# Eight or nine gather buffers beside three or two kept units of query weights

## The chip, the cores and the metric

The kernel runs on one core of a Trainium2 chip. The metric is the time of one execution on the device, in microseconds; the median of several runs is given.

## What is computed

Four decoder layers over 256 tokens of 1024 features, batch 1, all in float32. Each layer has a token mixer (HGRN2, FoX attention, Mamba-2 SSD, HGRN2 again) and then a PEER feed-forward: a query projection, a top-16 search over product keys, and 16 experts for each of 8 heads, each expert being one row of a table `u` and one row of a table `v`. The feed-forward is where the kernel spends its memory traffic:

```python
def peer_ffn(h, w_q, sub_keys, u_tab, v_tab):
    ...
        q = (xb @ w_q).reshape(M, PEER_HEADS, 2, PEER_HALF)
        s = jnp.einsum('mhcd,hckd->mhck', q, sub_keys).astype(jnp.float32)
        sv, si = lax.top_k(s, PEER_TOPK)
        ...
        idx = jnp.take_along_axis(cand_i, pos, axis=-1)
        gates = jax.nn.softmax(top_s, axis=-1)
        u = jnp.take(u_tab, idx, axis=0)
        v = jnp.take(v_tab, idx, axis=0)
        act = jax.nn.gelu(jnp.einsum('md,mhkd->mhk', xb, u).astype(jnp.float32), approximate=False) * gates
        return jnp.einsum('mhk,mhkd->md', act.astype(xb.dtype), v)
```

Every one of 256 tokens in 4 layers needs 8 x 16 rows of `u` and as many of `v`, 4 KB each.

## The kernel before

**Stages.** The tokens are two blocks of 128, so there are eight stages `s` (layer `s // 2`, block `s % 2`). In stage `s` the main loop (L1340) does the expert part of stage `s` in 64 pairs, and in between, a few instructions at a time, the "side" work that prepares stage `s + 1`: norm, mixer, norm, queries (`ready`, L1247). How much side work goes into each pair is paced by `SIDE` and `SPAN`.

**Gathers.** The host has joined `u` and `v` row by row, so one gather (`fetch`, L1210) brings 128 rows of 8 KB, 1 MB, by an indirect DMA that POOL issues, into one of `NGB` buffers `GB[n % NGB]`. A pair `i` uses gathers `2i` and `2i + 1`. For each, VectorE multiplies the `u` half with the repeated activations and sums (`dot`, L1221, in place in the buffer), ScalarE applies gelu and the gate (`spread`, L1227), and TensorE multiplies a diagonal-like 128x64 weight with the `v` half into the accumulator (L1241). With that matmul the buffer is free. `fetches(i)` (L1215), called at the head of pair `i`, issues all gathers up to number `2 i + NGB - 1`; on the chip each then waits for its buffer. There are 1024 gathers.

**Weights.** All other weights come in units of 1 MB (128 x 2048 floats) in one order, `stream` (L258), issued by SyncE in `loads` (L276): the mixer's units, then eight units `wq` of the layer's query weights, for each block again. A unit goes, first match, to a kept place if it is one of the first `NKEPT` query units of a layer, to a home, or to one of `NRAW` = 3 ring slots; when no slot is free, loading stops until a unit is used up (`half`, L314). A kept unit is loaded for the first block of a layer and found in place for the second, so it is read from memory once in a layer, any other query unit twice.

**Homes.** Before the first gather the gather buffers are empty, so some units of the start (numbers in `stream`; 20 to 27 are the query units of stage 0) are loaded there (`homes`, L265). A gather into such a buffer waits until TensorE has used the unit. The hand-written `order` (L267) tells in which order the first units are loaded.

**Memory.** Everything large lies in one arena (L181): `kept` takes `NKEPT` x 2048 floats of each partition and `gb` takes `NGB` x 2048.

**Engine helpers.** VectorE's instructions are all recorded at L203, most of ScalarE's at L216, matmuls of the projections at L238, transposes at L242.

Of the kernel before, what the change touches and what calls it, by code (L numbers as in the profile page):

```python
# [25 lines left out]
HALF = UNIT // 2  # L26
TOPK = 16
NQ = TOPK // 2
NGB = 8
NRAW = 3  # L30
MIX = 10464
STAGES = 2 * DEPTH
NKEPT = 3

FREE = {"hg": 0, "fox": 64 + 8 * T + 2 * D, "ssd": 352 + 4 * D + 96}
SPACE = 7 * D + P
# [128 lines left out]
def trunk(ctx: ExitStack, tc: tile.TileContext, d: dict, out: bass.AP):  # L165
# [14 lines left out]
    fst = cpool.tile([P, P + 8 * 2 * DEPTH], F32, name="fst")  # L180
    sizes = (("h", 2 * D), ("xT", D), ("XR", 2 * D), ("keys", UNIT), ("SS", 2048), ("mix", MIX), ("kept", NKEPT * UNIT),  # L181
             ("gb", NGB * 2 * D))
    arena = cpool.tile([P, sum(n for _, n in sizes)], F32, name="arena")
# [8 lines left out]
    SS = at_["SS"].rearrange("p (h c k) -> p h c k", h=8, c=2)  # L192
    GB = [at_["gb"][:, i * 2 * D:(i + 1) * 2 * D] for i in range(NGB)]
    mix = at_["mix"]
# [67 lines left out]
            stream += [(nm, i) for i in range(UNITS[KIND[l] if KIND[l] != "ssd" else "ssm"])]  # L262
            stream += [("wq%d" % l, i) for i in range(8)]

    homes = {3: GB[0], 4: GB[1], 17: GB[0], 18: GB[1], 19: GB[2], 23: GB[5], 24: GB[6]}  # L265
    homes.update({28 + i: mix[:, o:o + UNIT] for i, o in enumerate((SPACE, D, 3 * D))})
    order = [0, 1, 2, "rest", *range(3, 9), 23, 9, 10, 11, 24, 12, 13, 14, 22, 15, 16, "x", 17, 20, 18, 21, 19, "keys",  # L267
             "factors", 28, 25, "heads", 29, 26, 27, "states", 30]
# [7 lines left out]
    def loads():  # L276

        while order:
# [11 lines left out]
            else:  # L290
                nm, i = stream[u]
                keep = nm[0] == "w" and i < NKEPT
                if keep:
# [916 lines left out]
    def fetch(n):  # L1210
        (s, hh, q), g = pairs[n // 2], n % 2
        nc.gpsimd.indirect_dma_start(GB[n % NGB], None, d["uv"],  # L1212
                                     bass.IndirectOffsetOnAxis(ap=got[s, hh][0][:, g, q:q + 1], axis=0))

    def fetches(n):  # L1215

        while sent[0] < 2 * len(pairs) and sent[0] < 2 * n + NGB and pairs[sent[0] // 2][:2] in got:
            fetch(sent[0])
            sent[0] += 1

    def dot(i, g):  # L1221
        if g == 0:
            acts[i] = wk2.tile([P, 3, 2], F32, name="dots", bufs=4)
        u = GB[(2 * i + g) % NGB][:, 0:D]
        stt(u, u, 1.0, XR[:, g], op0=OP.mult, op1=OP.mult, accum_out=acts[i][:, 0, g:g + 1])

    def spread(i):  # L1227
# [10 lines left out]
        for e in range(2):  # L1238
            for g in range(2):
                v = GB[(2 * i + g) % NGB][:, D + e * 512:D + (e + 1) * 512]  # L1240
                nc.tensor.matmul(accs[s][e][g * 64:g * 64 + 64], dg[:, g], v, start=hh == 0 and q == 0,  # L1241
# [146 lines left out]
```

## Time and profile before

| | |
|---|---|
| median of 3 runs | 3226.96 us (3226.89 to 3229.7) |
| the profiled execution | 3229.51 us, of which the span of its instructions is 3227.4 us |
| mean granted TensorE clock | 0.897 |
| gathers (software queue) | 1073.81 MB in 147456 packets, 80.7% of the DMA engines' time |
| weights and the rest (hardware queue) | 247.23 MB in 35136 packets, 18.6% |
| query units loaded | 52 (38 into ring slots, 14 into the arena) |

The first gather is issued 118.1 us after the start of the span, the last at 3201.0 us. All rows with an arrow `out<-in` name tiles of the program; `arena<-in_uv,ix` is a gather. A row of the waits names the waiting engine, what it was about to do, what ended the wait, and the total in us, the times and the longest.

### The profile page before, as it was taken

Reading aid. Unit: us, or ns where it says so; the run is one execution under the profiler, and the core shown is the slowest. Engines: PE = TensorE matmul, PEld = TensorE weight load, DVE = VectorE, ACT = ScalarE, POOL = GpSimd, SP = SyncE. Lnnn points to the kernel's source line nnn. Section 1 sums busy time; section 2 is a strip of 40 time slices with the busy share of each in tenths; the row PEclk is TensorE's granted clock in tenths of the full one; section 3 lists DMA queues with packets and bytes.
Section 4 is the critical chain, followed back from the end, with each engine's and each line's share of the span. In section 5 each row is a group of like instructions: output and inputs, shape, how many; then the busy total and the mean of one; then the engine's idle time right before and its main releaser. Section 6 shows DMA issues by size and latency. Waiting matters only on the chain.

```text
span 3227.4 us, 30827 instructions
## 1 busy us (share of the span) xinstructions
PE 2482.3 (77%) x8604; PEld 1105.2 (34%) x8604; DVE 2117.9 (66%) x5583; ACT 1352.6 (42%) x3893; POOL 1178.7 (37%) x1030
## 2 busy tenths in 40 slices
PE   9888787777677786898778897778776777876565
PEld 4433233233233432344233443333323333332222
DVE  2576657566666866778567876576666667667764
ACT  3353334253334533477234673354433544333332
POOL 0243334333343433343333333343333433344442
PEclk9999898898889998999889998999988899887777
DMA  8899999999999999999999999999999999999997
GB/s 312 346 421 421 421 418 418 421 418 411 420 415 421 401 420 421 417 420 405 414 414 419 420 419 407 417 418 421 415 418 417 408 421 419 415 405 421 418 416 330
DMA packets 182760, 1322.99 MB, mean 410 GB/s; under 512 B 20288, under 2 KB 20672, under 8 KB 21824
## 3 DMA queue, kind: packets, MB, share of 16 engines
q0 software_dynamic: 147456, 1073.81, 80.7%
q1 hardware_dynamic: 35136, 247.23, 18.6%
q8 instruction: 71, 1.16, 0.1%
q14 instruction: 97, 0.79, 0.1%
HBM read 1319.90 MB, written 1.05 MB: 409 GB/s over the span
## 4 chain that ended last, share of the span: by engine, by line
DMA 57%; PE 15%; DVE 10%; issue 10%; ACT 4%; POOL 3%; POOLq 0%; SPq 0%; DVEq 0%; ACTq 0%
DMA arena<-in_uv,ix 57%; DVE arena L203 8%; PE acc L1241 8%; PE pj L238 5%; POOL arena L1212 3%; PE ps L238 2%; ACT dots L216 2%; ACT L216 1%; ACT dg L216 1%; PE ps L242 1%; ACT arena L216 0%; DVE eq L203 0%; DVE si L203 0%; DVE ti L203 0%; DVE af L203 0%
## 5 line engine op out<-in xcount | busy, mean ns | idle before, releaser
L203 DVE SCALAR_TENSOR_TENSOR arena<-arena 128x1024 f32<-128x1024 f32 (+3 forms) x1282 | 1321.7, 1048 | 910.7 <-DMA arena<-in_uv,ix 861.9
L1212 POOL DMA_INDIRECT arena<-in_uv,ix x1024 | 1176.6, 1149 | 2022.7 <-PE acc L1241 1437.8
L1241 PE MATMUL acc<-arena,dg 128*64 128x512 f32 x4096 | 1304.0, 724 | 720.7 <-ACT dg L216 719.0
L1241 PEld LDWEIGHTS acc<-arena,dg 128*64 128x64 f32 x4096 | 480.7, 156 | 1355.9 <-ACT dg L216 1043.9
L238 PE MATMUL pj<-raw,arena 128*128 128x512 f32 x1648 | 774.3, 612 | 5.2 <-DMA raw<-in_ssm 3.2
L216 ACT ACTIVATE dots<-dots 128x2 f32<-128x2 f32 x512 | 103.6, 202 | 1545.3 <-DVE arena L203 1544.5
L238 PEld LDWEIGHTS pj<-raw,arena 128*128 128x128 f32 x1648 | 302.3, 194 | 484.6 <-issue 467.1
L216 ACT ACT_TABLE_LOAD x325 | 417.0, 1283 | 6.7 <-DVE arena L203 0.8
L216 ACT ACTIVATE dg<-m,dots 128x64 f32<-128x64 f32 x1024 | 292.5, 333 | 0.0
L216 ACT ACTIVATE dots<-dots,gs 128x1 f32<-128x1 f32 x1024 | 245.6, 286 | 16.7
L238 PE MATMUL ps<-arena 128*128 128x128 f32 (+3 forms) x992 | 129.4, 287 | 1.8 <-ACT arena L1078 0.9
L238 PE MATMUL pj<-arena 128*128 128x512 f32 (+1 forms) x288 | 125.2, 582 | 0.3 <-DVE arena L203 0.3
L238 PEld LDWEIGHTS ps<-arena 128*128 128x128 f32 (+2 forms) x992 | 102.4, 168 | 67.1 <-issue 40.8
L242 PEld LDWEIGHTS ps<-fst,arena 128*128 128x128 f32 x568 | 67.2, 146 | 88.1 <-issue 43.4
L242 PE MATMUL ps<-fst,arena 128*128 128x128 f32 x568 | 91.5, 288 | 6.9 <-DVE arena L203 4.1
L216 ACT ACTIVATE arena<-arena 128x512 f32<-128x512 f32 (+3 forms) x132 | 67.7, 555 | 43.9 <-DVE arena L203 41.4
L203 DVE DVE_READ_ACCUMULATOR arena<-arena 128x1 f32 x1024 | 84.0, 82 | 0.0
L238 PEld LDWEIGHTS pj<-arena 128*128 128x128 f32 x288 | 53.1, 192 | 70.1 <-issue 58.8
L203 DVE FIND_INDEX8 si<-sv,arena 128x8 uint32<-128x128 f32 x256 | 69.7, 284 | 0.0
L203 DVE MAX8 sv<-arena 128x8 f32<-128x128 f32 x256 | 61.7, 282 | 10.4 <-ACT arena L1082 5.7
L238 PE MATMUL ps<-cst,arena 128*128 128x128 f32 (+3 forms) x288 | 66.8, 360 | 0.0
L203 DVE COPY gs<-ig 64x16 f32<-64x16 f32 (+1 forms) x256 | 52.5, 205 | 4.7
(113 smaller groups left out, 1227.2 us busy)
## 6 DMA issues: line engine op xcount, KB each, us to landing
raw<-in_hg SPq DMA_DIRECT2D x72, 1024.0 KB, 9.2
raw<-in_ssm SPq DMA_DIRECT2D x64, 1024.0 KB, 9.3
raw<-in_wq SPq DMA_DIRECT2D x38, 1024.0 KB, 9.6
raw<-in_fox SPq DMA_DIRECT2D x32, 1024.0 KB, 9.1
arena<-in_uv,ix POOLq DMA_INDIRECT x1024, 15.3
arena<-in_wq SPq DMA_DIRECT2D x14, 1024.0 KB, 14.9
arena<-in_hg SPq DMA_DIRECT2D x8, 1024.0 KB, 13.3
arena<-in_keys SPq DMA_DIRECT2D x4, 1024.0 KB, 9.3
```

Source lines behind the costliest of these rows:

```text
L203: return getattr(nc.vector, name)(o, *a, **k)
L216: nc.scalar.activation(o, i, f, **k)
L238: nc.tensor.matmul(o, w, m, start=start, stop=stop)
L242: nc.tensor.transpose(o, i, ident)
L1212: nc.gpsimd.indirect_dma_start(GB[n % NGB], None, d["uv"], bass.IndirectOffsetOnAxis(ap=got[s, hh][0][:, g, q:q + 1], axis=0))
L1241: nc.tensor.matmul(accs[s][e][g * 64:g * 64 + 64], dg[:, g], v, start=hh == 0 and q == 0, stop=hh == 7 and q == NQ - 1)
```

## The change

`NGB` goes from 8 to 9 and `NKEPT` from 3 to 2, so the arena keeps its size: 2048 floats of each partition go from `kept` to `gb`. The third query unit of each layer now goes through the ring of three slots in both blocks, and at the start, as number 22 of the stream, to a home in a gather buffer; the homes of units 23 and 24 move up by one buffer, as the program lists them.

```diff
-NGB = 8
+NGB = 9
 NRAW = 3
 MIX = 10464
 STAGES = 2 * DEPTH
-NKEPT = 3
+NKEPT = 2
...
-    homes = {3: GB[0], 4: GB[1], 17: GB[0], 18: GB[1], 19: GB[2], 23: GB[5], 24: GB[6]}
+    homes = {3: GB[0], 4: GB[1], 17: GB[0], 18: GB[1], 19: GB[2], 22: GB[5], 23: GB[6], 24: GB[7]}
```

## The prediction

> **What bounds the kernel now.** I read the top of the page, the DMA rate cut by stage, then the same view cut around the dips in that rate, and last how long a gather takes to land inside and outside a dip. The page first (section 2's rows are 40 equal slices of 80.7 us):
>
> ```profile
> span 3227.4 us, 30827 instructions
> PE 2482.3 (77%) x8604; PEld 1105.2 (34%) x8604; DVE 2117.9 (66%) x5583; ACT 1352.6 (42%) x3893; POOL 1178.7 (37%) x1030
> DMA  8899999999999999999999999999999999999997
> ...
> DMA packets 182760, 1322.99 MB, mean 410 GB/s; under 512 B 20288, under 2 KB 20672, under 8 KB 21824
> DMA arena<-in_uv,ix 57%; DVE arena L203 8%; PE acc L1241 8%; PE pj L238 5%; POOL arena L1212 3%; PE ps L238 2%; ACT dots L216 2%; ACT L216 1%; ACT dg L216 1%; PE ps L242 1%; ACT arena L216 0%; DVE eq L203 0%; DVE si L203 0%; DVE ti L203 0%; DVE af L203 0%
> ```
>
> No engine is busy more than 77%, the DMA engines are busy in every slice, and the chain that ends last spends 57% of the span in gathers. So the time is a start, the bytes divided by a rate, and a tail. The next view cuts the DMA-fed part into the eight stages; columns are the stretch, its length, the busy time of PE, PEld, DVE, ACT and POOL, the granted clock, the DMA share and GB/s.
>
> ```profile
> 132.00:511.00 379.00, 303.33 (x997) 127.38 (x999) 253.00 (x665) 156.47 (x452) 141.53 (x126) 0.90 1.01 420
> 511.00:895.00 384.00, 282.26 (x1011) 127.24 (x1009) 248.44 (x674) 151.02 (x473) 145.54 (x130) 0.89 1.01 417
> 895.00:1273.00 378.00, 288.99 (x1056) 132.23 (x1053) 254.24 (x674) 156.68 (x474) 147.55 (x129) 0.91 1.01 416
> 1273.00:1698.00 425.00, 344.68 (x1212) 155.52 (x1209) 299.91 (x823) 217.11 (x572) 150.82 (x127) 0.92 1.01 414
> 1698.00:2117.00 419.00, 345.71 (x1273) 159.62 (x1271) 298.41 (x812) 211.43 (x561) 151.21 (x129) 0.94 1.01 416
> 2117.00:2511.00 394.00, 299.19 (x1028) 130.29 (x1027) 254.58 (x653) 159.63 (x461) 146.52 (x130) 0.90 1.01 417
> 2511.00:2891.00 380.00, 296.87 (x1041) 129.47 (x1039) 254.03 (x653) 159.11 (x458) 151.52 (x130) 0.90 1.01 413
> 2891.00:3200.00 309.00, 188.15 (x527) 73.70 (x522) 206.29 (x505) 93.68 (x345) 134.30 (x122) 0.77 1.01 419
> ```
>
> An undisturbed stretch stands at 421 GB/s, which I take as the ceiling of this kernel's mix:
>
> ```profile
> 140.00:400.00 260.00, 211.32 (x699) 87.58 (x697) 175.71 (x468) 117.40 (x322) 95.63 (x84) 0.92 1.01 421
> ```
>
> Each stage's shortfall is its length times (421 - rate)/421: 0.9, 3.6, 4.5, 7.1, 5.0, 3.7, 7.2 and 1.5 us, together 33.5 us. That is everything that a better fed DMA can give back between 132 and 3200 us. Seven dips hold much of it:
>
> ```profile
> 700.00:760.00 60.00, 40.92 (x134) 18.14 (x134) 33.34 (x89) 20.14 (x70) 18.70 (x18) 0.86 1.00 409
> 1051.00:1104.00 53.00, 43.47 (x202) 22.77 (x201) 44.61 (x125) 35.64 (x100) 23.51 (x21) 0.94 0.99 392
> 1440.00:1540.00 100.00, 89.69 (x349) 42.59 (x348) 83.62 (x212) 66.83 (x155) 33.80 (x28) 0.95 1.00 403
> 1600.00:1640.00 40.00, 40.00 (x137) 16.60 (x137) 21.32 (x51) 12.31 (x43) 14.99 (x14) 1.00 1.00 405
> 1894.00:1961.00 67.00, 62.75 (x265) 31.28 (x265) 58.74 (x140) 50.31 (x113) 21.23 (x19) 0.95 0.99 399
> 2490.00:2562.00 72.00, 53.34 (x222) 25.00 (x222) 51.35 (x131) 35.47 (x98) 33.48 (x28) 0.88 1.00 404
> 2836.00:2861.00 25.00, 19.82 (x77) 8.47 (x75) 15.47 (x42) 7.64 (x27) 11.61 (x11) 0.93 0.95 366
> ```
>
> By the same formula they lack 1.7, 3.6, 4.3, 1.5, 3.5, 2.9 and 3.3 us, 20.8 us in 417 us; the other 12.7 us lie in small dips. How a gather lives in the quiet stretch (140 to 400 us) and, below it, in a dip (2490 to 2535 us): its issues, then issue to landing:
>
> ```profile
> L1212 POOL DMA_INDIRECT arena<-in_uv,ix x84: 932/937/1978, 144.2 to 395.0; - x84
> DMA to landing us min/median/max: 9.2/17.5/21.7
> ```
>
> ```profile
> L1212 POOL DMA_INDIRECT arena<-in_uv,ix x19: 932/938/1824, 2490.2 to 2534.6; - x19
> DMA to landing us min/median/max: 10.4/12.7/15.1
> ```
>
> In the quiet stretch a gather starts every 260/84 = 3.10 us, so eight buffers turn once in 24.8 us, of which 17.5 us are DMA: the data waits in a queue. Between 2490 and 2535 few weight loads compete, a gather starts every 45/19 = 2.37 us, eight turn in 18.9 us, and 12.7 us of that is DMA. The rest of the turn, some 6 to 7 us, is the way from landing through dot, gelu and matmul to the next issue. In a dip the ring is therefore too short: the DMA runs out of gathers to work on. What holds POOL before a gather over the whole run says the same:
>
> ```profile
> POOL arena L1212 <- PE acc L1241: 1437.8, 424, 9.2
> POOL arena L1212 <- DVE arena L203: 262.6, 74, 8.5
> POOL arena L1212 <- DVE ts L203: 13.6, 4, 5.1
> ```
>
> It waits for a buffer (the matmul of L1241 that reads it last); waits that end with the routing's own instructions are a few us.
>
> **The change part by part.**
>
> Added bytes. Each layer streams its eight query units twice, and a kept one is loaded once. With two kept, unit 2 is loaded again in the second pass of each of four layers: four loads more, 52 becoming 56. The loads and what a load is:
>
> ```profile
> raw<-in_wq SPq DMA_DIRECT2D x38, 1024.0 KB, 9.6
> arena<-in_uv,ix POOLq DMA_INDIRECT x1024, 15.3
> arena<-in_wq SPq DMA_DIRECT2D x14, 1024.0 KB, 14.9
> ```
>
> 1024 KB is 1.0486 MB, at 421 GB/s 2.49 us; four are +10.0 us, as nothing hides a byte where the DMA is the bound. If they fell wholly into dips they would cost 0, the lower end; the upper end is 10.0.
>
> [...] I use 2.49.
>
> Ninth buffer. The number of gathers (1024), their POOL instructions and the order of DVE, ACT and PE stay. One more gather is in flight whenever the DMA is the bound, and a stretch of busy engines must last 2.49 us longer before the DMA starves. Two ways to size it. First, at most one buffer per dip: min(shortfall, 2.49) over the seven is 1.7 + 2.5 + 2.5 + 1.5 + 2.5 + 2.5 + 2.5 = 15.7, and the small dips, each far under 2.49, return whole, 12.7: 28.4 us. Second, a dip limited by the ring alone speeds up by 9/8, capped at 421: 392 would be 441, 399 would be 449, only 366 stays below, at 412; nearly all 33 us return. Against both stand the stretches in which PE is itself the bound (40.00 of 40 us at 1600, 62.75 of 67 at 1894, 89.69 of 100 at 1440): the buffer shifts their start once and the engine is still full. I halve their 1.5 + 2.5 + 2.5 and take 28.4 - 3.3 = 25 us. The ends: 0 if one more buffer leads to no more in flight, 9.2 if only the four dips with PE under 85% return theirs and no small one does, 33.5 if all returns.
>
> Start. Homes move: units 22, 23, 24 lie in buffers 5, 6, 7 instead of kept, 5, 6. Gathers 5 and 6 waited for PE:
>
> ```profile
> 127.13 0.94 POOL L1212 DMA_INDIRECT arena<-in_uv,ix  x1 [2.95 <-PE pj L238]
> 130.56 1.21 POOL L1212 DMA_INDIRECT arena<-in_uv,ix  x1 [2.50 <-PE pj L238]
> ```
>
> ```profile
> 124.00:140.00 16.00, 13.01 (x33) 5.55 (x32) 11.39 (x35) 4.66 (x13) 5.23 (x6) 0.89 1.01 422
> ```
>
> Now 5 waits for unit 22, 6 for 23, 7 for 24, each one unit earlier, so up to 2.95 us earlier. The DMA already runs at 422 from 124 to 140, so this is 0. If that cover were gone it would be a gain of at most 2.95. Gather 7, which waits for no unit today, now waits for unit 24, that is until the 130.56 of today's gather 6: covered by the same DMA work.
>
> Weight ring. Unit 2 now takes one of three raw slots. POOL and DVE wait for none of it; behind a late unit on PE stand the matmuls of L1241 and so the buffers. SyncE's timeline in a query stretch has two loads, each issued as a unit is used up:
>
> ```profile
> 2036.73 6.72 SPq L303 DMA_DIRECT2D raw<-in_wq  x2
> ```
>
> So a unit comes about every 6 us, and a slot's reload, issued when the unit three earlier is done, has some 12 us (two units between) before its use, of which landing takes 9.6. Cost 0, unless loads become later (a rival below).
>
> Sum, against the profiled execution's 3229.51 us (span 3227.4, 2.1 around it): 3229.5 + 10.0 - 25 = 3214.5. The median of runs is 2.5 lower, so **3212 us**.
>
> **The rivals.**
>
> A, the engines hold the dips, not the ring. Speaking for it: the PE-full rows above, three of the seven dips. Speaking against: 2490 to 2562 has PE at 53.34 of 72 and DVE at 51.35, and is starved all the same. Then 9.2 us come back and 10.0 go: 3227 - 9.2 + 10 = 3228 us.
>
> B, on the slower side: weight loads queue behind the deeper ring of gathers. The place is the output projection of the SSD layer, where PE already meets its loads:
>
> ```profile
> PE pj L238 <- DMA raw<-in_ssm: 3.2, 2, 2.0
> ```
>
> ```profile
> DMA to landing us min/median/max: 8.9/9.1/10.2
> ```
>
> ```profile
> DMA to landing us min/median/max: 9.1/9.7/10.4
> ```
>
> (The first is the view of waits: us in total, times, longest. The last two rows are landings of raw loads from 140 to 400 and 2490 to 2562.) If a load landed one gather, 2.49 us, later, about five units in each of two SSD passes would stall PE by that, 25 us, and the 25 us regained would be eaten: 3227 + 10 = 3237 us. It decides from a median landing of raw loads over about 11.5 us. Against it: loads land in 9.1 us beside gathers that take 17.5 and in 9.7 beside gathers that take 12.7, so they do not stand behind them.
>
> C, the ninth gather is not in flight. POOL may be held by something else than the buffer: the index of a pair half a pair further ahead, or room for the descriptors. The 13.6 us on routing and the median of 937 and 938 ns of an issue in both stretches above speak against it. Then the loads are paid and nothing returns: again 3237 us.
>
> D, everything returns, and the start's 2.95 us too: 3227 + 10 - 33.5 - 3 = 3200.5 us. For it speaks the second way of sizing, against it the stretches with PE full.
>
> **How the numbers follow.** Forecast (15 to 33 us back, 3204 to 3222) 0.62; A 0.18; B 0.07; C 0.07; D 0.06. A measurement here can tell about 0.2%, 6.5 us, from no change. Forecast and D are faster by over that, except the forecast's edge above 3220.5, for which I take 0.02 off: 0.66; A and that edge are within, 0.20; B and C are slower, 0.14. The range from 3200 to 3236 takes in A and the low end of D and stops just short of B and C, so that about 0.15 is left out; the likeliest case alone is 3204 to 3222.
>
> **What would show it.** Bytes of 1327.2 MB and 56 query loads (right in any case). Gather landing about 2.5 us longer, 17.5 to 18 in the median over the run, with raw loads still at 9 to 10. Rates by stage at 419 to 421, the dips at 2490 and 2836 nearly closed, those at 1440 and 1894 smaller but there. POOL's wait for PE before a gather not changed much. I am wrong if landing grows and the rates by stage do not (A), if PE waits for raw loads by tens of us (B), or if landing stays at 15.3 (C).

## The result, and the profile after

| | before | after |
|---|---|---|
| median | 3227.59 us (3225.22 to 3231.54, 10 runs) | 3238.16 us (3235.32 to 3240.42, 10 runs) |
| ratio, 95% interval | | 1.003 [1.0022, 1.0039] |
| span of the profiled execution | 3227.4 us | 3237.2 us |

The change costs about 10.6 us where 15 us less were forecast: the four loads are paid and the ninth buffer returns nothing. The top of the page of the changed kernel, and the two rows of its DMA issues for the query units:

```profile
span 3237.2 us, 30838 instructions
PE 2485.4 (77%) x8604; PEld 1103.5 (34%) x8604; DVE 2118.3 (65%) x5583; ACT 1353.4 (42%) x3893; POOL 1182.0 (37%) x1030
DMA  8899999999999999999999999999999999999997
...
DMA packets 183336, 1327.19 MB, mean 410 GB/s; under 512 B 20352, under 2 KB 20736, under 8 KB 21888
...
raw<-in_wq SPq DMA_DIRECT2D x45, 1024.0 KB
...
arena<-in_wq SPq DMA_DIRECT2D x11, 1024.0 KB
```

There are 1327.19 - 1322.99 = 4.20 MB more, in 45 + 11 = 56 query loads. The mean rate is the 410 GB/s of before, so the span grows with the bytes. The same seven stretches that were the dips of before, in the changed kernel (columns as in the prediction, the last one GB/s):

```profile
700.00:760.00 60.00, 41.55 (x137) 17.77 (x135) 35.60 (x94) 22.24 (x75) 20.40 (x20) 0.89 1.01 420
1051.00:1104.00 53.00, 43.07 (x212) 23.94 (x210) 45.93 (x129) 36.25 (x104) 26.46 (x21) 0.97 0.99 400
1440.00:1540.00 100.00, 91.45 (x360) 44.59 (x359) 84.55 (x222) 71.08 (x166) 35.33 (x29) 0.97 1.01 417
1600.00:1640.00 40.00, 39.51 (x132) 16.28 (x131) 20.03 (x49) 11.59 (x41) 15.02 (x14) 1.00 1.01 417
1894.00:1961.00 67.00, 61.11 (x261) 30.45 (x259) 58.85 (x145) 49.53 (x111) 23.47 (x20) 0.97 1.00 408
2490.00:2562.00 72.00, 53.00 (x215) 25.10 (x213) 53.17 (x136) 35.80 (x100) 32.40 (x27) 0.84 1.00 407
2836.00:2861.00 25.00, 20.24 (x80) 9.35 (x80) 17.20 (x39) 11.69 (x35) 9.66 (x10) 1.00 1.01 414
```

By the formula of the prediction they lack 9.0 us where they lacked 20.8. Seen alone, this looks as forecast. But the stages do not follow:

```profile
132.00:511.00 379.00, 299.06 (x981) 126.54 (x983) 251.35 (x663) 155.43 (x449) 139.48 (x125) 0.92 1.01 421
511.00:895.00 384.00, 286.94 (x990) 126.50 (x988) 248.53 (x674) 150.13 (x471) 145.00 (x129) 0.88 1.01 420
895.00:1273.00 378.00, 282.95 (x1046) 129.65 (x1043) 253.59 (x673) 156.75 (x474) 148.88 (x128) 0.91 1.01 417
1273.00:1698.00 425.00, 352.49 (x1244) 158.45 (x1244) 299.77 (x823) 217.59 (x573) 151.16 (x129) 0.90 1.01 415
1698.00:2117.00 419.00, 346.12 (x1266) 159.34 (x1265) 297.68 (x809) 210.74 (x556) 150.30 (x127) 0.94 1.01 415
2117.00:2511.00 394.00, 299.57 (x1019) 130.09 (x1020) 254.91 (x652) 159.79 (x461) 147.45 (x129) 0.89 1.01 417
2511.00:2891.00 380.00, 296.60 (x1011) 126.87 (x1008) 252.53 (x647) 158.58 (x456) 150.55 (x128) 0.89 1.01 416
2891.00:3200.00 309.00, 182.67 (x552) 74.47 (x552) 206.02 (x507) 93.49 (x343) 133.45 (x121) 0.81 1.01 415
```

Against 420, 417, 416, 414, 416, 417, 413 and 419 of before, stages 0 and 1 gain 3.6 us, the next five stay within 3 GB/s, and the last one falls. What closed in the dips opened elsewhere. The whole fed part as one row, before and then after:

```profile
132.00:3200.00 3068.00, 2349.16 (x8112) 1035.47 (x8112) 2068.90 (x5453) 1305.13 (x3794) 1168.99 (x1017) 0.89 1.01 417
```

```profile
132.00:3200.00 3068.00, 2346.39 (x8096) 1031.93 (x8096) 2064.38 (x5445) 1302.50 (x3782) 1166.27 (x1013) 0.89 1.01 417
```

It is 417 GB/s in both (416.6 and 417.0, which is 3 us in 3068). The last stage lined up by its end, 317 us long, before and then after:

```profile
2891.00:3208.00 317.00, 192.44 (x542) 75.85 (x538) 209.99 (x511) 95.89 (x354) 135.90 (x123) 0.78 1.01 419
```

```profile
2901.00:3218.00 317.00, 184.86 (x516) 73.44 (x512) 209.21 (x509) 95.68 (x353) 133.47 (x121) 0.81 1.00 412
```

The deeper ring is early at first and pays it back at the end, which points at something with one constant pace under both. Two waits, from the view of waits and the row of TensorE's projections of the changed kernel, exclude others:

```profile
POOL arena L1212 <- PE acc L1241: 1440.1, 422, 9.5
```

```profile
L238 PE MATMUL pj<-raw,arena 128*128 128x512 f32 x1704 | 800.2, 612 | 3.9 <-DMA raw<-in_ssm 1.8
```

POOL still waits for a buffer, as before (1437.8 us), and TensorE waits for weight units no more than it did.

**What the landings hid.** A gather raises its semaphore (the counter by which a transfer reports that it is done) 16 times: the trace of before has 16 increments for 1023 of its 1024 gathers. A gather also has 16 packets of 4 bytes beside its 128 of 8 KB (131072 and 16384 packets on its queue in that trace). I read the increments as one from each of the 16 DMA engines; the landing time of the profile's rows is the last of the 16. Read one by one from the trace's semaphore records, averaged over a stage without its first ten gathers and without those of which the trace lacks an increment (one with eight buffers, 174 with seven, 197 with nine), in mean us behind the first increment:

```
               15th increment, stages 1 to 7        16th increment, stages 1 to 7
7 buffers      2.66 2.57 2.97 2.64 2.51 2.19 1.83   3.97 3.44 4.55 3.65 3.55 3.63 3.03
8 (before)     2.14 2.26 2.85 2.83 2.72 2.52 2.18   6.93 6.76 7.85 7.60 7.48 6.65 5.09
9 (after)      4.24 2.32 3.01 2.71 2.54 2.20 1.95   9.30 9.46 11.01 10.81 10.85 10.11 8.14
```

(Seven buffers are the second run below.) From stage 2 on 15 of the 16 come within about 3 us of each other at any depth, and the last comes 2 to 4 us later for each added buffer. I read this as a queue at one engine: what a deeper ring adds waits there, and the buffers that it holds keep the other engines from going on. The first increment stays where it was (in stage 5, 9.59 us after the issue before and 9.42 after), so the landing grows by what the last one does, there from 17.07 to 20.27 us. How that engine falls behind, in the last stage of before:

```
gather   16th increment   16th - 10th   15th - 10th   step of the 16th from the gather before
  931        2980.6           4.02          2.08         2.48
  932        2983.1           4.03          2.08         2.49
  933        2985.6           4.02          2.07         2.49
  934        2989.1           4.99          2.07         3.45   an 8 KB packet of queue q14 starts at 2985.8
  935        2991.6           5.00          2.06         2.49
  936        2994.1           5.01          2.06         2.49
```

The lag stands to 0.01 us, then jumps by 0.97 us and stands again; between jumps the last engine keeps one pace, a gather of 1 MB in 2.49 us. The records do not name the engine; that it is one and the same is inferred from the lag that stands. The jump falls together with a packet of q14. In the page's list of DMA queues (packets, MB, share), of before and after alike, there are two queues of the kind "instruction":

```profile
q8 instruction: 71, 1.16, 0.1%
q14 instruction: 97, 0.79, 0.1%
```

The packets of q8 are 16 KB each, those of q14 8 KB. Whose instructions they carry is not in the records; I infer it from counts. I take the 71 on q8 for TensorE's instructions (18388 recorded, 259 to a packet) and those on q14 for blocks of 128 instructions of the other engines: 5820 recorded for VectorE, 4089 for ScalarE, 2062 for POOL and 468 for SyncE make 97.2 blocks. The runs with added instructions, below, agree: 8064 more of TensorE's brought 32 packets on q8 (252 each), and 2048 more of VectorE's or POOL's brought 16 on q14 (128 each). At the time of a packet, the engine whose block it is should stand at about the same place within its 128 instructions each time; 47 packets find VectorE between 48 and 63, where an even spread would put 12. Where the place leaves one engine alone, the lag around the packet changes by a median of +0.98 us for VectorE (23 blocks), 0.00 for ScalarE (15) and 0.02 for POOL (9), and by -0.02 for TensorE's 67 packets on q8. VectorE's median stays at 0.97 to 0.98 however the places are cut. Those of ScalarE and POOL rest on few blocks and move with the cut, up to 0.9, so the sorting alone does not clear these two. VectorE's 45 blocks by 0.98 us are 44 us, of the order of the 33.5 us of shortfall.

### The profile page after: what moved, and what is told of

It is laid out like the page before. It is cut to its first block, busy times and chain, and to the rows that moved or that the text cites. A ratio compares the mean times of both kernels' runs of the same rounds, so it can differ in the third digit from the quotient of the medians.

```text
span 3237.2 us, 30838 instructions
## 1 busy us (share of the span) xinstructions
PE 2485.4 (77%) x8604; PEld 1103.5 (34%) x8604; DVE 2118.3 (65%) x5583; ACT 1353.4 (42%) x3893; POOL 1182.0 (37%) x1030
## 2 busy tenths in 40 slices
DMA packets 183336, 1327.19 MB, mean 410 GB/s; under 512 B 20352, under 2 KB 20736, under 8 KB 21888
## 4 chain that ended last, share of the span: by engine, by line
DMA 62%; PE 14%; issue 9%; DVE 9%; ACT 4%; POOL 3%; POOLq 0%; SPq 0%; DVEq 0%; ACTq 0%
DMA arena<-in_uv,ix 62%; PE acc L1241 8%; DVE arena L203 7%; PE pj L238 4%; POOL arena L1212 3%; PE ps L238 2%; ACT dots L216 2%; ACT dg L216 1%; ACT L216 1%; ACT arena L216 0%; PE ps L242 0%; DVE eq L203 0%; DMA raw<-in_hg 0%; DVE si L203 0%; DVE sv L203 0%
## 5 line engine op out<-in xcount | busy, mean ns | idle before, releaser
L238 PE MATMUL pj<-raw,arena 128*128 128x512 f32 x1704 | 800.2, 612 | 3.9 <-DMA raw<-in_ssm 1.8
L238 PEld LDWEIGHTS pj<-raw,arena 128*128 128x128 f32 x1704 | 312.0, 193 | 500.1 <-issue 484.5
L216 ACT ACT_TABLE_LOAD x325 | 417.0, 1283 | 6.7 <-DVE arena L203 0.8
L238 PE MATMUL pj<-arena 128*128 128x512 f32 (+1 forms) x232 | 98.2, 571 | 0.3 <-DVE arena L203 0.3
L238 PEld LDWEIGHTS pj<-arena 128*128 128x128 f32 x232 | 42.4, 190 | 53.9 <-issue 41.7
```

The lines of the kernel that those rows point to most:

```text
L216: nc.scalar.activation(o, i, f, **k)
L238: nc.tensor.matmul(o, w, m, start=start, stop=stop)
```

## The experiments

The expectations carry theories by letter. T says that one DMA engine sets the pace and that the ring's depth therefore buys nothing; T2 is T with the cause named: the fetch of VectorE's instructions. Each kernel ran beside the kernel before on the same chip; 1 us is 0.00031 of a ratio.

**The loads without the buffer.** Two kept units, the new homes, eight buffers.

```diff
-NKEPT = 3
+NKEPT = 2
...
```

> Eight buffers, two kept units: the four added loads alone. Theory T (one of the 16 DMA engines carries more than the others, is never idle and sets the pace; the ring only decides how far the other 15 run ahead of it): the loads cost 4 x 2.49 = 10.0 us and the ninth buffer was worth nothing, so 3237 us, the same as the changed kernel within 3 us. Theory R (as predicted: the ring is what starves, and the ninth buffer gave back much): without it the time is 3245 us or more. Theory E (engines hold the dips, one buffer gives back some 9 us): 3246 us.

Measured: 1.003 [1.0018, 1.0041], span 3238.4 us. This is the whole change in its ratio and nearly in its span, so the ninth buffer returns nothing that these runs can show (the two intervals leave some 5 us), and the loads cost their 10 us.

**The ring the other way.** Seven buffers, three kept units.

```diff
-NGB = 8
+NGB = 7
```

> Seven buffers, three kept units, no load added: one buffer fewer than before. T: the pace-setting DMA engine still has work waiting, so 3227 us plus at most one buffer's time, 3227 to 3230. R: every stretch without weight loads turns seven buffers in the time of eight, so the lost 33 us of DMA time at least double, 3255 us or more. E: the dips grow by one buffer's time each, 3227 + 7 x 2.5 = 3244 us.

Measured: 1.0007 [0.9998, 1.0016]. A buffer fewer costs at most some 5 us, and the 16th increment comes 2 to 4 us closer to the first (first row of the table above). A ring that is too short, as the prediction read it, would have lost tens of us.

**Less work for one engine.** Thirteen loads (the expectation counts 14) were split into 120 and 8 partitions, meant to leave the last of the 16 engines out.

```diff
-                    nc.sync.dma_start(r, d[nm][i])
+                    if u > 30 and u % 15 == 0:
+                        nc.sync.dma_start(r[0:120], d[nm][i][0:120])
+                        nc.sync.dma_start(r[120:P], d[nm][i][120:P])
+                    else:
+                        nc.sync.dma_start(r, d[nm][i])
```

> Before, with 14 of the weight loads (every fifteenth unit) issued as two transfers, partitions 0 to 119 and 120 to 127, so that a split over 15 DMA engines may leave one of them out of most of the load. T, if the engine left out is the slow one: it loses 14 x 8 rows of 0.309 us = 34.6 us of work, so 3227 - 30 = 3197 us, give or take 6. T, if the slow engine is one of the others: no gain, 3227 to 3233. R and E: the bytes are the same, 3227 us.

Measured: 1.0194 [1.018, 1.0208], 62 us over, 4.8 us for each of the 13 split loads; no theory had that. A stretch around one of them:

```profile
320.00:360.00 40.00, 27.48 (x106) 12.91 (x102) 24.70 (x65) 12.89 (x36) 11.93 (x10) 0.83 1.01 370
```

The same stretch of before has 421 GB/s. The split load is issued at 332.3 us, and from 336 to 344 us the 8 KB packets of all transfers take a median of 550 to 600 ns instead of 312, so the loss is not in one engine. Why it comes was not tried. The run says nothing about which engine lags, and that stays open.

**Is it TensorE's instruction fetch?** The first version of T put the lag down to q8, whose packets are the longest (a median of 1.07 us in the trace of before, where those of 8 KB take 0.31). Four matmuls of one column with zero weights per pair, added into the accumulator (in all pairs but the last of a stage):

```diff
...
+            for _ in range(4):
+                nc.tensor.matmul(accs[s][0][0:64, 0:1], zer, ..., start=False, stop=False)
```

> Before, with four matmuls of one column and zero weights added to each pair's accumulation: some 8000 TensorE instructions more, no byte of data. T with the fetch of TensorE's instructions as the extra work (71 blocks of 16 KB on one queue now, each putting one DMA engine back by about 0.55 us): 31 blocks more, 3227 + 17 = 3244 us. If TensorE's instructions do not matter: its own time grows by under 1 us a pair of 6 us, hidden beside the DMA, 3227 to 3232 us.

Measured: 1.0002 [0.9993, 1.0011]. Page rows:

```profile
PE 2611.3 (81%) x12636; PEld 1433.8 (44%) x12636; DVE 2117.2 (65%) x5584; ACT 1352.2 (42%) x3893; POOL 1174.9 (36%) x1030
...
q8 instruction: 103, 1.69, 0.2%
```

32 more blocks and 129 us more of TensorE's time cost nothing. That version falls, and no trace shows the 0.55 us a block that its expectation reckoned with. The sorting of q14's packets by engine then led to T2.

**VectorE's fetch, and POOL's beside it.** Four memsets of one column per pair, 2048 in all, 16 blocks, once on VectorE and once on POOL.

```diff
...
+            for j in range(4):
+                nc.vector.memset(pad[:, j:j + 1], 0.0)
```

> Before, with four VectorE memsets of one column added to each pair, 2048 instructions and no byte of data. Theory T2 (the DMA engine that lags is the one that also fetches VectorE's instructions; in the trace of before its lag jumps by 0.98 us at each 8 KB block of 128 VectorE instructions): 16 blocks more, 16 x 0.98 = 15.7 us more, a ratio of 1.005 to before. If VectorE's instructions do not matter to the DMA: 2048 x 0.07 us of VectorE time in a VectorE that is busy two thirds of the time, hidden: 0 to 2 us.

> The same 2048 memsets on POOL. T2: POOL's instruction blocks do not move the lag of the slow DMA engine in the trace, so 0 to 3 us, a ratio of 1.000 to 1.001. If any added instruction or its fetch costs DMA time: as much as on VectorE, about 1.005.

Measured on VectorE: 1.0063 [1.0049, 1.0076], 20 us. On POOL: 0.9996 [0.9987, 1.0005]. The pages, VectorE first:

```profile
PE 2492.0 (77%) x8604; PEld 1103.5 (34%) x8604; DVE 2137.2 (66%) x7631; ACT 1353.0 (42%) x3893; POOL 1164.1 (36%) x1030
...
q14 instruction: 113, 0.93, 0.1%
```

```profile
PE 2491.0 (77%) x8604; PEld 1104.1 (34%) x8604; DVE 2122.3 (66%) x5583; ACT 1352.7 (42%) x3893; POOL 1282.6 (40%) x3078
...
q14 instruction: 113, 0.93, 0.1%
```

The same 16 packets more on the same queue cost 20 us when they are VectorE's and nothing when they are POOL's. Nor did VectorE's memsets hold up the issue of the gathers: POOL's instruction takes a mean of 1135 ns with them and 1149 ns before. One loose end: VectorE's busy time grew by 19.3 us, nearly as much as the time. The last run takes that up.

**Trading buffers for kept units.** If depth is free, loads can be saved with it: seven buffers and four kept units, and six and five (homes cut to match).

```diff
-NGB = 8
+NGB = 7
-NKEPT = 3
+NKEPT = 4
...
```

> The change turned round: seven buffers, four kept units, the same memory. T (the pace is one DMA engine's work, seven buffers suffice): four loads fewer, -10.0 us, and 0 to 2 us for the shorter ring, so 8 to 10 us under before, a ratio of 0.997. R (the ring starves): over 20 us above before.

> Six buffers, five kept units. Eight loads fewer, -20 us. T: with seven buffers the slow engine's lag behind the 15th was down to 1.7 us of the 4.6 with eight, 2.9 us a buffer; with six no lag is left, the slow engine itself must run dry at times, and part or all of the 20 us is lost: between 18 us under and 15 us over before. R: far slower, 1.02 or more.

Measured with seven: 0.9989 [0.998, 0.9998], 3.6 us less, where the four saved loads are worth 10. With six: 1.0297 [1.0283, 1.0311], beyond what T allowed; here the reading of the prediction (R, 1.02 or more) was the right one. Its fed part:

```profile
132.00:3200.00 3068.00, 2326.08 (x7968) 1023.28 (x7966) 2018.70 (x5352) 1280.93 (x3692) 1101.20 (x980) 0.88 0.99 401
```

With six the 16th increment comes 2.1 to 2.9 us behind the first, within 0.8 us of the 15th: the slow engine's queue holds hardly more than the others', and now the ring does starve the DMA, at 401 GB/s. So T holds down to seven buffers and not below. With seven the ring may already limit in places: with four kept units one of the 40 slices stands at 393 GB/s, where before it stood at 418.

**Fewer VectorE instructions.** The dot product without its sum (`accum_out`), and so without the separate instruction that reads the sum, 1024 of them. Gelu takes the first product in place of the sum, straight from the gather buffer. So the layers compute something else and later layers gather other rows; the run is for the time alone.

```diff
-        stt(u, u, 1.0, XR[:, g], op0=OP.mult, op1=OP.mult, accum_out=acts[i][:, 0, g:g + 1])
+        stt(u, u, 1.0, XR[:, g], op0=OP.mult, op1=OP.mult)
...
-        act(a[:, 1], a[:, 0], AF.Gelu)
+        act(a[:, 1], at_["gb"].rearrange("p (n x) -> p n x", n=NGB)[:, 2 * i % NGB:2 * i % NGB + 2, 0], AF.Gelu)
```

> Before, with the sum of each dot product left out: the multiplication over 1024 columns stays, its accumulator output goes, and gelu reads the first product. That removes 1024 of VectorE's instructions (the reading of the accumulator), 8 blocks of 128, and no byte of data. T2: 8 blocks at the 0.98 us of the lag's jumps, or at the (1.0063 x 3232 - 3232)/16 = 1.3 us that added blocks cost, so 8 to 10 us less, a ratio of 0.997. If VectorE's instructions were not the slow DMA engine's burden: VectorE's 84 us of reading accumulators are hidden now, 0 to 2 us less.

Measured: 0.997 [0.9959, 0.9982], 10 us less.

```profile
PE 2484.4 (77%) x8604; PEld 1100.4 (34%) x8604; DVE 2107.5 (65%) x4559; ACT 1353.0 (42%) x3893; POOL 1184.4 (37%) x1030
```

With the waits among them, which the page does not count as busy, the trace has 4809 instructions of VectorE where there were 5820, and 512 more of ScalarE, four blocks, and the gain is there all the same.

**The same work on another engine.** Nine small copies, casts and scalings per head of the routing moved from VectorE to ScalarE.

```diff
-        vec.tensor_copy(sf, si)
+        nc.scalar.copy(sf, si)
...
-                vec.tensor_copy(gs[o, g], igv[i, :, :, j])
+                nc.scalar.copy(gs[o, g], igv[i, :, :, j])
```

> Before, with nine small copies, casts and scalings of the routing of each head moved from VectorE to ScalarE: 576 instructions, 4.5 blocks, leave VectorE and as many come to ScalarE. T2: 4.5 x 1.0 to 1.3 us, 4 to 6 us less, a ratio of 0.9985, if ScalarE's waits for VectorE hold nothing up. Otherwise 0, or more where ScalarE, which now waits in the middle of a routing, comes late with the gelu.

Measured: 0.9987 [0.9979, 0.9996], 4 us less. With the seven-buffer kernel above, whose interval overlaps with it, this is the fastest version that keeps the sums, ahead of both the kernel before and the changed one.

```profile
PE 2486.5 (77%) x8604; PEld 1098.5 (34%) x8604; DVE 2021.2 (63%) x5012; ACT 1452.6 (45%) x4464; POOL 1168.8 (36%) x1030
```

VectorE lost 97 us of busy time and 599 instructions (571 that count as busy, and 28 waits); ScalarE gained 811, 6.3 blocks. The time followed VectorE's instructions, at about 1 us for 128.

**Both together.** The moved copies with seven buffers and four kept units.

> Both: the moved instructions with seven buffers and four kept units. T2: the 5.5 us of e7 and the 4 to 6 us of e10 add, a ratio of 0.997. If with seven buffers the ring is the limit in places, less of it: 0.998 to 0.999.

Measured: 0.9992 [0.9983, 1.0002]. The two do not add. The expectation's second case, a ring that already limits in places, would fit, but that was not tried.

**Instructions or busy time?** One memset of 128 columns per pair on VectorE, in place of four of one column.

```diff
-            for j in range(4):
-                nc.vector.memset(pad[:, j:j + 1], 0.0)
+            nc.vector.memset(pad, 0.0)
```

> The kernel before with one VectorE memset of 128 columns per pair, at the place where the run with 2048 memsets had four of one column: 512 instructions, that is 4 blocks of 128, but by the 138 ns of a 96-column memset and the 485 ns of a 512-column one some 165 ns each, about 84 us of VectorE time where the 2048 short ones made 19.3 (2137.2 - 2117.9). It tells two readings apart that the earlier runs left side by side, since there the time rose and fell by nearly the busy time of VectorE that was added or removed (+20 us for +19.3, -10 us for -10.4). Theory T2 (what costs is the fetch of VectorE's instructions at the lagging DMA engine, about 1 us a block): 4 to 5 us slower, ratio 1.001 to 1.002. Rival V (VectorE's busy time is on the path that sets the end): 84 us slower, ratio 1.026. Rival W (VectorE's work in each pair delays the buffer's way back to the ring, partly hidden): 20 us or more, ratio 1.006 or above.

Measured: 1.0018 [1.0009, 1.0027], 5.8 us.

```profile
PE 2490.8 (77%) x8604; PEld 1100.8 (34%) x8604; DVE 2169.3 (67%) x6095; ACT 1352.6 (42%) x3893; POOL 1176.5 (36%) x1030
```

```profile
L1359 DVE MEMSET pad<- 128x128 f32 x512 | 84.5, 165 | 0.0
```

VectorE is busy 51.4 us longer than before, far more than the 19.3 us of the short memsets, and the time grows by less than a third as much. The four runs that changed VectorE's part, side by side (1 us of ratio by the 3232 us, or here 3227 us, of before; instructions with the waits):

```
                    instructions  blocks of 128   VectorE busy   time, 95% interval       us per block
2048 short memsets     +2048          +16           +19.3 us     +20.4 (15.8 to 24.6)        1.3
512 long memsets        +512           +4           +51.4 us      +5.8 (2.9 to 8.7)          1.5
copies moved            -599           -4.7         -96.7 us      -4.2 (-6.8 to -1.3)        0.9
no sum                 -1011           -7.9         -10.4 us      -9.7 (-13.3 to -5.8)       1.2
```

The time goes by the number of instructions, not by the busy time.

The increments show the same inside each trace. From the last increment of the first gather of stage 1 (number 128) to that of gather 1000, I take off 2.491 us (1 MB at 421 GB/s) for every MB that landed, and set what is left beside VectorE's instructions in that time:

```
                             us left   VectorE blocks   us per block
seven buffers                  36.4         38.5            0.95
eight buffers (before)         36.7         38.5            0.95
nine buffers (after)           36.8         38.4            0.96
no sum                         30.4         31.7            0.96
copies moved                   33.1         34.5            0.96
512 long memsets               38.7         41.9            0.92
2048 short memsets             56.0         52.2            1.07
more TensorE instructions      41.7         38.6            1.08
more POOL instructions         40.9         38.5            1.06
six buffers, five kept units  142.5         38.6            3.69
```

Read at 0.95 us a block, the rows down to the last but one agree to some 6 us. Seven, eight and nine buffers leave the same 36 to 37 us, which is the direct sign that depth does not change the pace; with six the loss is of another kind.

## Why the prediction was wrong

**The loads: right.** 10.0 us by 2.49 us each; the run with the loads alone has the change's own 1.003, an interval of 6 to 13 us, and the span of the change grew by 9.8 us.

**Start and weight ring: right.** Up to 132 us the DMA moves 307 GB/s where it moved 309, the first stage then runs at 421 GB/s, and TensorE's wait for `raw<-in_ssm` is 1.8 us. Rival B is out.

**The ninth buffer: wrong, the step that failed.** The prediction put 25 us on this step, from "In a dip the ring is therefore too short: the DMA runs out of gathers to work on." What it took from the rows was right as far as it went: landings of 12.7 us in a dip and 17.5 us in the quiet stretch. But a landing is the last of 16 increments. The other engines did run dry at times: counted from the start and duration of each packet, fewer than 16 are under way in 10% of the dip from 2490 to 2562 us and in 34% of that from 2836 to 2861, and never in the quiet stretch. The last engine, as I read the lag, still had work: in the two dips the 16th increment comes a mean of 3.5 and 3.4 us behind the 15th. It had lost about 1 us (a median of 0.98) to each of VectorE's instruction blocks and did not catch up, since between jumps it takes the same 2.49 us a gather as the first 15. The mean rate and the mean busy share average over 16 engines and cannot show this. So the step that failed is the ring as the cause of the shortfall, and in its place stands one engine's pace, at 36 to 37 us left with seven, eight or nine buffers. Two sums then followed from the wrong cause, and their agreement (28.4 and nearly 33 us) proved nothing, since both took the shortfall as the ring's to return. The quiet 421 GB/s was also read amiss as a rate that could last: the other engines were still running ahead there, which the ring's depth allows once. The last increment comes 1.4 us behind the tenth at 140 us and 6.8 us at 450 us. The ninth buffer lengthened that run (stages 0 and 1 gain 3.6 us) and it was paid back in the last stage, at 412 GB/s where 419 stood before.

**The rivals.** C had the outcome, nothing back and 3237 us, but not the mechanism: the ninth gather was in flight and landed late at the one engine. The test written for A, a landing that grows with stage rates that do not, was the sign that appeared; the price of A, 9.2 us back, was not. The full engines of A do not set the rate either: TensorE with 129 us more of work cost nothing (1.0002), and VectorE with 51.4 us more cost 5.8 us. None of the cases held a single DMA engine as the bound, and the range was drawn to end just short of C.

**The lag and the instructions.** One of the 16 increments lags (7.48 us behind the first where the 15th is 2.72 behind, stage 5 of before), and the runs tie the lag to VectorE's instructions: more of them cost time (1.0063 with 16 blocks), more of TensorE's (1.0002 with 32) or POOL's (0.9996 with 16) none that these runs can show.

**What stays open.** Which physical engine it is; why a block whose packet takes a median of 318 ns puts it back by three times that; and whether ScalarE's and POOL's blocks are free because other engines, which have slack, carry them. No run tried these. That VectorE's blocks pass through the lagging engine is itself inferred, from the jumps and from the runs that added and removed instructions.

## What to carry to other kernels

When the DMA is the bound and its rate falls short, look at the spread of the 16 completions of a transfer before lengthening its ring: here the last one lagged the rest and stayed behind, and depth only moved the wait. Then count instructions as well: here VectorE's were on the path at about 1 us for 128 of them, although VectorE was idle a third of the time. And try a ring smaller before making it larger: seven buffers gave 1.0007 here, within the noise, and six (with fewer loads) 1.0297.

## What the runs showed of the hardware

Splitting a 128-partition load of 1 MB into 120 and 8 partitions cost 4.8 us, about twice the 2.49 us that the load takes at full rate; in the one looked at, the packets of all transfers took a median of 550 to 600 ns instead of 312 for some 8 us. And instruction fetch, 0.1% of the DMA engines' time on the page in each of its two queues, was worth, as I read it, more than 1% of this kernel's time: VectorE's 45 blocks by 0.98 us are 44 of 3227 us, an estimate from the jumps of the lag, of which the run without the sums took back 10 us with eight blocks.
